# A two-layer encoder with 32 experts per layer: the experts' token lists are loaded three experts ahead, and two small steps beside the experts change place

## The chip, the cores and the metric

The kernel runs on one core of one Trainium2 chip. A core has a matrix engine (TensorE, PE in the profile; its weight loads are PEld), a vector engine (VectorE, DVE), a scalar engine (ScalarE, ACT), a general engine (GpSimd, POOL) that also issues the indirect DMAs, and SyncE (SP), which issues the large loads. Each engine works off its own instructions in order; semaphores tie them together. The metric is the device time of one execution in microseconds: 5532.35 us before the change, the median of three runs (5514.12, 5542.82, 5532.35).

## The reference

The input is x, 4096 tokens of 1024 float32. Two layers follow one another. Each has a mixer over positions (layer 0: retention in two directions and windowed attention; layer 1: a Fourier transform over positions and channels), then a layer norm, then a mixture of experts, then a layer norm:

```
x   = layer_norm(alpha * x + mixer(x))
g   = top-1 of 4 groups (softmax of x @ w_coarse + b_coarse)
e   = top-2 of the 8 experts of group g (x @ w_fine + b_fine)
ffn = sum over the two experts: gate_e * ((silu(x @ w_gate_e) * (x @ w_up_e)) @ w_down_e)
x   = layer_norm(alpha * x + ffn)
```

There are 32 experts per layer, each with a hidden width of 512. Every token goes through two of them, so an expert sees some 128 to 430 tokens.

## The kernel before

The program runs two sweeps for the mixer of layer 0, then the experts of layer 0 (class `Experts`, layer 0), the Fourier mixer, and the experts of layer 1, with the class `Done` beside them. The change touches only `Experts` and `Done`.

**What the lists are.** The router leaves in DRAM, for each expert, a list of (row of the token, gate). `Experts.index` (L1507) loads the list of one expert into a small tile `idx` by a plain DMA issued from GpSimd; there is a ring of three such tiles. `Experts.gather` (L1514) fetches 128 token rows into `xg` by an indirect DMA whose offsets are in `idx`. `Experts.scatter` (L1605) adds a finished tile `yo` to the rows of the accumulator `acc_d` in DRAM, again with offsets of `idx`; two scatters follow each other only when the earlier one has landed.

**One expert.** `Experts.expert(e)` (L1613) writes out the order of work by hand. It begins with what is left of expert e-1: the second half of its output product for tile 1 and that tile's scatter (the function `pending`). Then it issues `index(e+1)` and the gathers of expert e+1 on GpSimd. Then come the 32 steps of `gate_up` (L1540): four blocks j of eight steps k, each step six matmuls of expert e's weights `w` against the transposed tokens `xt`. Block j writes the PSUM tile `pgu[j % 2]`, so block 2 needs block 0 to have been read, and block 3 (its first weights are `w6`) needs block 1 to have been read: by a ScalarE silu (L1556) and a VectorE product (L1557) into `hid`. Then `down` (L1564) multiplies the hidden values by the output weights, and between its products the transposes of expert e+1's gathered tokens (`trans`, L1518) are woven in.

**The weights.** Each expert has 12 chunks of 512 KB. SyncE loads them into a ring of four `raw` tiles; `split` (L1492) turns a chunk into a high part (ScalarE) and a low part (VectorE) at fixed steps: 0, 2, 4, 6 for the current expert's last four chunks, then steps 1 and 3 of blocks 1 to 3 for the next expert's chunks 0 to 5 (`w0` to `w5`), and the rest within `down`. ScalarE and VectorE work in order, so a late chunk holds whatever stands behind its split.

**Finished tokens (layer 1 only).** `Done` normalizes and writes out tokens whose experts are all behind. Its steps are placed by (expert, step) in `Done.plan` (L1244). In experts 0 to 7, `count` (L1279) copies four columns to the bf16 tile `lb` on VectorE; `ranks` (L1283) multiplies them on TensorE and works out places `ddsti` on VectorE; `write` (L1299) issues four indirect DMAs on GpSimd, each of which waits for the one before it to land. From expert 8 on, `Done.gather` fetches a finished tile, `stats` (VectorE, then two small GpSimd instructions, L102 and L1332) finds mean and deviation in `dst`, `scale` (ScalarE, L1335) waits for them, `gain` (GpSimd, L1338), `bias` (VectorE) and `store` (GpSimd) follow.

Of the kernel before, what the change touches and what calls it, by code (L numbers as in the profile page):

```python
# [9 lines left out]
I32 = mybir.dt.int32  # L10
# [4 lines left out]
P = 128  # L15
# [4 lines left out]
E = 32  # L20
# [1192 lines left out]
class Done:  # L1213
# [30 lines left out]
    def plan(s):  # L1244

        put = lambda e, h, f, *a: s.at.setdefault(e, {}).setdefault(h, []).append(lambda: f(*a))
        for e in range(8):
            for h, f in ((9, s.count), (16, s.ranks), (22, s.write)):
                put(e, h, f, 4 * e)
        put(7, 23, s.counts)  # L1250
        put(8, 20, s.load)

        def tile(k, i, b, eg, hg, ec, hc, at=(0, 8, 10, 14, 16)):
            ix = s.ix[:, sum(CAPS[:k]) + i, :]
            put(eg, hg, s.gather, ix, b)
            for d, f in zip(at, (s.stats, s.scale, s.gain, s.bias, s.store)):
                put(ec, hc + d, f, ix, b)
        for k in range(3):
            es = range(8 * k + 8, 8 * k + 16 if k < 2 else 29)
            for i in range(CAPS[k]):  # L1260
                j, e = i // len(es), es[i % len(es)]
                tile(k, i, e % 2 + 2 * j, e, 28 + j, e + 1, 8 + 4 * j)
        for i in range(2):
            tile(3, i, 2 * i, 30, 12 + i, 30, 20 + 3 * i)
        for i, b in enumerate((1, 3, 4)):
            tile(3, 2 + i, b, 30, 28 + i, 31, 1 + 2 * i, (0, 5, 6, 11, 12))
        for i in range(2):
            tile(4, i, 2 * i, 31, 12, 31, 18 + i, (0, 8, 14, 24, 25))
# [168 lines left out]
class Experts:  # L1437
# [8 lines left out]
    def __init__(s, T, layer, sp, pp):  # L1446
        s.T, s.nc, s.tc = T, T.nc, T.tc
        s.layer, s.slots = layer, SLOTS[layer]
        w = max(s.slots)
        s.listed = sum(T.listed[layer][-2:], [])  # L1450
        s.x, s.acc, s.lst, s.cnt = T.x1_d[layer], T.acc_d[layer], T.lst_d[layer], T.cnt[layer]
        s.wgu, s.wd = T.A["wgu"][layer], T.A["expert_w_down"][layer]
        pair = lambda n, sh: (sp.tile(sh, F32R, name=n + "h"), sp.tile(sh, F32R, name=n + "l"))
        s.raw = [sp.tile([P, 1024], F32, name=f"raw{i}") for i in range(s.NRAW)]
        s.w = [pair(f"w{i}", [P, 1024]) for i in range(12)]
        s.nt = -(-w // P)
        s.xg = [sp.tile([P, D], F32, name=f"xg{i}") for i in range(s.nt)]
        s.xt = pair("xt", [P, 8, w])
        s.idx = [sp.tile([P, s.nt, 2], I32, name=f"idx{i}") for i in range(3)]
        s.lidx = sp.tile([P, 2, 2], I32, name="lidx")  # L1460
        s.hid = [sp.tile([P, w], F32, name=f"hid{i}") for i in range(2)]
        s.ht = pair("ht", [P, 4, w])
        s.tail = sp.tile([P, 4, 128], F32R, name="tail")
        s.yo = [sp.tile([P, D], F32, name=f"yo{i}") for i in range(2)]
        s.ylo = sp.tile([64, 512], F32, name="ylo")
        s.over = sp.tile([1, E], F32, name="over")
        s.cap = sp.tile([1, E], F32, name="cap")
        s.more = sp.tile([1, 1], I32, name="more")
        s.pgu = [pp.tile([P, 2, 512], F32, name=f"pgu{i}") for i in range(2)]
        s.pt = [pp.tile([P, 512], F32, name=f"pt{i}") for i in range(2)]  # L1470
        s.py = [pp.tile([P, 512], F32, name=f"py{i}") for i in range(2)]
        s.nload = s.nsplit = 0
        s.c = dict.fromkeys(("pt", "py"), 0)
        s.done = Done(T, sp, s.acc, s.nxt, s.raw) if layer else None
# [26 lines left out]
    def rows(s, e, t):  # L1501
        return max(0, min(P, s.slots[e] - t * P))
# [2 lines left out]
        return range(-(-s.slots[e] // P))  # L1505

    def index(s, e):  # L1507
        ix = s.idx[e % 3]
        n = len(s.tiles(e))
        d = s.nc.gpsimd.dma_start(ix[:, 0:n, :], s.lst[e * LS:e * LS + n * P, :].rearrange("(t p) c -> p t c", p=P))  # L1510
        if e == 0:
            s.T.after(d, s.listed)
# [99 lines left out]

    def expert(s, e):  # L1613

        ix, size = s.idx[e % 3], s.slots[e]
        rows = lambda t: s.rows(e, t)
        late = [f for t in s.tiles(e) if t > 1 for f in s.trans(t, rows(t))] if e else []
        pend, s.pend = s.pend, None
        if pend:
            at = {}  # L1620
            for i, f in enumerate(late):
                at.setdefault(i if len(late) > 2 else 2 * i + 1, []).append(f)
            pend(at)
        more = e + 1 < E
        steps = []
        if more:
            ix2 = s.idx[(e + 1) % 3]
            s.index(e + 1)
            for t in s.tiles(e + 1):
                s.gather(ix2, t, s.rows(e + 1, t))  # L1630
            steps = [f for t in range(2) for f in s.trans(t, s.rows(e + 1, t))]
        at = [{2 * i: [s.split] for i in range(4)}]
        at += [{1: [s.split], 3: [s.split]} for _ in range(3)]
        side = {h: list(f) for h, f in s.done.at.get(e, {}).items()} if s.done else {}
        if e == 2:
            side.setdefault(13, []).append(s.excess)
        if s.last(e):
            for t in s.tiles(e):
                side.setdefault(20, []).append(lambda t=t: s.done.fetch(ix, t, t, rows(t)))
        for h in [h for h in side if h < 32]:  # L1640
            at[h // 8].setdefault(h % 8, []).extend(side.pop(h))
        for j in range(4):
            s.gate_up(j, size, at[j])
        steps = [s.split] + steps[:3] + [s.split] + steps[3:]
        at = {2 * i: [f] for i, f in enumerate(steps[:4])}
        for h in [h for h in side if h < 40]:
            at.setdefault(h - 32, []).extend(side.pop(h))
        yo = s.yo[0]
        if s.last(e):
            m = rows(2)  # L1650
            yo0 = s.done.x[4]
            s.down(yo0, ix, 0, at=at)
            s.done.adds(yo0, 0, P, 0)
            if m:
                s.down(s.yo[1], ix, 2, m)
            side = [f for h in sorted(side) for f in side[h]]
            for f in side:
                f()
            first0, second0 = s.done.final_steps(yo0, 0, P)
            first0()  # L1660
            if m:
                s.done.adds(s.yo[1], 2, m, 2)
                first2, second2 = s.done.final_steps(s.yo[1], 2, m)
                first2()
            s.down(yo, ix, 1, rows(1), last=True)
            second0()
            s.done.final(yo, 1, rows(1))
            if m:
                second2()
            return  # L1670
        order = [0, *(t for t in s.tiles(e) if t > 1)]
        for i, t in enumerate(order):
            y = s.yo[(len(order) - i) % 2]
            s.down(y, ix, t, rows(t), at=at if t == 0 else {})
            s.scatter(y, ix, t, rows(t))
        s.down(yo, ix, 1, rows(1), (0,), at={i: [f] for i, f in enumerate(steps[4:])})
        for h in sorted(side):
            for f in side[h]:
                f()

        def pending(at={}):
            s.down(yo, ix, 1, rows(1), (1,), at)
            s.scatter(yo, ix, 1, rows(1))
        s.pend = pending
# [39 lines left out]
    def run(s):  # L1724
        nc, tc = s.nc, s.tc
        s.pend = None
        with tc.manual_schedule(engines=COMPUTE | {POOL}):
            s.index(0)
            nc.gpsimd.memset(s.ylo, 0.0)
            nc.scalar.copy(s.tail[0:64].rearrange("p k c -> p (k c)"), s.ylo)  # L1730
            nc.scalar.copy(s.tail[64:128].rearrange("p k c -> p (k c)"), s.ylo)
            for t in s.xg:
                nc.gpsimd.memset(t, 0.0)
            for t in s.tiles(0):
                s.gather(s.idx[0], t, s.rows(0, t))
            for _ in range(8):
                s.split()
            for t in s.tiles(0):
                for f in s.trans(t, s.rows(0, t)):
                    f()  # L1740
            nc.sync.dma_start(s.cap, s.T.A["c_slots"][s.layer:s.layer + 1, :])
            if s.done:
                s.done.setup()
            for e in range(E):
                s.expert(e)
            if s.pend:
                s.pend()
            if s.done:
                s.done.finish()
            s.rest()  # L1750
# [146 lines left out]
```

## Time and profile before

| what | value |
|---|---|
| median of three runs | 5532.35 us |
| the profiled execution's own time | 5520.84 us |
| its span (first to last instruction) | 5519.2 us |
| PE busy | 5089.8 us (92%) |
| DVE busy | 3413.6 us (62%) |
| ACT busy | 2382.1 us (43%) |
| POOL busy | 1636.5 us (30%) |
| mean granted TensorE clock | 0.957 |
| bytes moved | 907.96 MB, mean 165 GB/s |

The span is 1.6 us shorter than the execution's own time. Busy times are sums over the whole program; the stages differ, so the rows further down go by stage. The experts of layer 0 run from about 2100 to 3420 us of the span, those of layer 1 from about 4048 to 5476 us.

### The profile page before, as it was taken

Reading aid. Unit: us, or ns where it says so; the run is one execution under the profiler, and the core shown is the slowest. Engines: PE = TensorE matmul, PEld = TensorE weight load, DVE = VectorE, ACT = ScalarE, POOL = GpSimd, SP = SyncE. Lnnn points to the kernel's source line nnn. Section 1 sums busy time; section 2 is a strip of 40 time slices with the busy share of each in tenths; the row PEclk is TensorE's granted clock in tenths of the full one; section 3 lists DMA queues with packets and bytes.
Section 4 is the critical chain, followed back from the end, with each engine's and each line's share of the span. In section 5 each row is a group of like instructions: output and inputs, shape, how many; then the busy total and the mean of one; then the engine's idle time right before and its main releaser. Section 6 shows DMA issues by size and latency. Waiting matters only on the chain. (4 is left out here: it accounts for less than half of the span.)

```text
span 5519.2 us, 85268 instructions
## 1 busy us (share of the span) xinstructions
PE 5089.8 (92%) x32364; PEld 4607.6 (83%) x32364; DVE 3413.6 (62%) x7398; ACT 2382.1 (43%) x4310; POOL 1636.5 (30%) x1556
## 2 busy tenths in 40 slices
PE   9999999799999996999999997889859999999986
PEld 7888888599999986989999896779858888888876
DVE  6777777566666665555544453759855565555555
ACT  4555555322222214555545453643245455555443
POOL 1111111033333332221212121845632333332335
PEclk9999999799999998999999998999869999999998
DMA  4212121433333326777766675866467877777664
GB/s 155 63 59 67 55 67 48 146 103 103 113 100 112 104 89 213 237 218 221 206 183 197 185 238 160 257 206 219 174 195 206 216 226 245 213 212 207 205 212 146
DMA packets 312312, 907.96 MB, mean 165 GB/s; under 512 B 48596, under 2 KB 76420, under 8 KB 311796
## 3 DMA queue, kind: packets, MB, share of 16 engines
q1 hardware_dynamic: 249780, 709.44, 38.4%
q0 software_dynamic: 62096, 192.82, 15.0%
q8 instruction: 259, 4.24, 0.3%
q14 instruction: 177, 1.45, 0.1%
HBM read 678.13 MB, written 226.39 MB: 164 GB/s over the span
## 5 line engine op out<-in xcount | busy, mean ns | idle before, releaser
L1606 POOL DMA_INDIRECT acc_d<-yo,idx x154 | 275.5, 1789 | 1210.8 <-ACT yo L1587 723.4
L83 PE MATMUL pj<-w1h,xh 128*128 128x512 f32 (+1 forms) x1024 | 396.7, 387 | 7.0 <-ACT w1h L78 6.5
L84 PE MATMUL pj<-w1l,xh 128*128 128x512 f32 (+1 forms) x1024 | 378.4, 370 | 2.4 <-DVE w1l L79 2.3
L85 PE MATMUL pj<-w1h,xl 128*128 128x512 f32 (+1 forms) x1024 | 377.0, 368 | 0.0
L1515 POOL DMA_INDIRECT xg<-x_d,idx x157 | 167.7, 1068 | 508.3 <-issue 292.9
L133 PE MATMUL pt<-ident,xg 128*128 128x128 f32 x1256 | 201.5, 286 | 109.7 <-DMA xg<-x_d,idx 61.5
L133 PEld LDWEIGHTS pt<-ident,xg 128*128 128x128 f32 x1256 | 163.4, 148 | 163.7 <-DMA xg<-x_d,idx 64.0
L79 DVE TENSOR_TENSOR xtl<-pt,xth 128x512 fp32r<-128x512 f32 (+12 forms) x314 | 184.9, 598 | 180.8 <-ACT xth L78 179.3
L83 PE MATMUL pj<-w2h,xh 128*128 128x384 f32 (+1 forms) x768 | 265.3, 346 | 9.4 <-DVE rb L212 9.1
L83 PE MATMUL po<-woh,cath 128*128 128x354 f32 (+1 forms) x768 | 262.5, 342 | 2.9 <-ACT cath L78 2.0
L1587 ACT ACTIVATE yo<-py,idx 128x512 f32<-128x512 f32 (+6 forms) x256 | 175.8, 687 | 206.6 <-PE py L85 192.3
L85 PE MATMUL po<-woh,catl 128*128 128x354 f32 (+1 forms) x768 | 254.6, 332 | 5.4 <-DVE catl L79 4.2
L78 ACT ACTIVATE hth<-hid 128x256 fp32r<-128x256 f32 (+11 forms) x256 | 104.6, 408 | 351.8 <-DVE hid L1557 343.5
L84 PE MATMUL pj<-w2l,xh 128*128 128x384 f32 (+1 forms) x768 | 251.8, 328 | 3.4 <-DVE w2l L79 3.3
L84 PE MATMUL po<-wol,cath 128*128 128x354 f32 (+1 forms) x768 | 253.3, 330 | 0.0
L85 PE MATMUL pj<-w2h,xl 128*128 128x384 f32 (+1 forms) x768 | 251.2, 327 | 0.0
L78 ACT ACTIVATE ph<-tr 128x384 fp32r<-128x384 f32 (+1 forms) x256 | 122.6, 479 | 286.4 <-PE tr L133 283.6
L1556 ACT ACTIVATE hid<-pgu 128x272 f32<-128x272 f32 (+22 forms) x256 | 97.5, 381 | 336.2 <-PE pgu L1552 330.7
L79 DVE TENSOR_TENSOR pl<-tr,ph 128x384 fp32r<-128x384 f32 (+1 forms) x256 | 139.0, 543 | 134.3 <-ACT ph L78 130.5
L85 PEld LDWEIGHTS pj<-w1h,xl 128*128 128x128 f32 x1024 | 194.3, 190 | 32.7
L1557 DVE TENSOR_TENSOR hid<-hid,pgu 128x272 f32<-128x272 f32 (+22 forms) x256 | 107.8, 421 | 177.2 <-ACT hid L1556 171.7
L78 ACT ACTIVATE xth<-pt 128x512 fp32r<-128x512 f32 (+12 forms) x314 | 161.1, 522 | 126.9 <-PE pt L133 125.3
(507 smaller groups left out, 18688.3 us busy)
## 6 DMA issues: line engine op xcount, KB each, us to landing
raw<-in_wgu SPq DMA_DIRECT2D x512, 512.0 KB
raw<-in_expert_w_down SPq DMA_DIRECT2D x256, 512.0 KB
xraw<-in_xT SPq DMA_DIRECT2D x64, 512.0 KB
acc_d<-xacc SPq DMA_DIRECT2D x64, 512.0 KB
x<-x_d SPq DMA_DIRECT2D x32, 530.0 KB
xres<-in_x SPq DMA_DIRECT2D x32, 512.0 KB
x_d<-tres SPq DMA_DIRECT2D x32, 512.0 KB
fx<-acc_d SPq DMA_DIRECT2D x32, 512.0 KB
```

Of the source, the lines that this page charges most:

```text
L78: self.nc.scalar.activation(hi, src, AF.Copy)
L79: self.nc.vector.tensor_sub(lo, src, hi)
L83: mm(out, xh, wh, start=start, stop=False)
L84: mm(out, xh, wl, start=False, stop=False)
L85: mm(out, xl, wh, start=False, stop=stop)
L133: self.nc.tensor.transpose(pt[:, k * P:(k + 1) * P], src[:, k * P:(k + 1) * P], self.ident)
L1515: s.nc.gpsimd.indirect_dma_start(out=s.xg[t][0:m, :], out_offset=None, in_=s.x, in_offset=bass.IndirectOffsetOnAxis(ap=ix[0:m, t, 0:1], ax ...
L1556: nc.scalar.activation(hid, ps[:, 0, 0:n], AF.Silu)
L1557: nc.vector.tensor_mul(hid, hid, ps[:, 1, 0:n])
L1587: s.nc.scalar.activation(yo[0:m, w], py[i][0:m, :], AF.Copy, scale=gate)
L1606: s.nc.gpsimd.indirect_dma_start(out=s.acc, out_offset=bass.IndirectOffsetOnAxis(ap=ix[0:m, t, 0:1], axis=0), in_=yo[0:m, :], in_offset=No ...
```

## The change

The list of expert e+3, no longer that of expert e+1, is loaded in `expert(e)`, and it is issued ahead of what is left of expert e-1, no longer behind it. The ring has five tiles. The lists of experts 1 and 2 are loaded before the first expert, behind the gathers of expert 0. In `Done.plan`, `count` moves from step 9 to step 2, `ranks` from 16 to 20, `write` from 22 to 26, and the last `counts` from 23 to 27, so that `lb` is made 18 steps ahead of its use (before: 7).

```diff
-            for h, f in ((9, s.count), (16, s.ranks), (22, s.write)):
+            for h, f in ((2, s.count), (20, s.ranks), (26, s.write)):
                 put(e, h, f, 4 * e)
-        put(7, 23, s.counts)
+        put(7, 27, s.counts)
...
-        s.idx = [sp.tile([P, s.nt, 2], I32, name=f"idx{i}") for i in range(3)]
+        s.idx = [sp.tile([P, s.nt, 2], I32, name=f"idx{i}") for i in range(5)]
...
     def index(s, e):
-        ix = s.idx[e % 3]
+        ix = s.idx[e % 5]
...
     def expert(s, e):
-        ix, size = s.idx[e % 3], s.slots[e]
+        ix, size = s.idx[e % 5], s.slots[e]
         rows = lambda t: s.rows(e, t)
         late = [f for t in s.tiles(e) if t > 1 for f in s.trans(t, rows(t))] if e else []
         pend, s.pend = s.pend, None
+        if e + 3 < E:
+            s.index(e + 3)
         if pend:
...
         if more:
-            ix2 = s.idx[(e + 1) % 3]
-            s.index(e + 1)
+            ix2 = s.idx[(e + 1) % 5]
             for t in s.tiles(e + 1):
                 s.gather(ix2, t, s.rows(e + 1, t))
...
             for t in s.tiles(0):
                 s.gather(s.idx[0], t, s.rows(0, t))
+            s.index(1)
+            s.index(2)
             for _ in range(8):
                 s.split()
```

## Rows read from the trace of the kernel before

**Rows 1.** Busy time by stretch: length, engines' busy us (instructions), granted clock, DMA share, GB/s.
```profile
2120.00:3380.00 1260.00, 1250.90 (x8478) 1140.06 (x8478) 648.11 (x843) 651.96 (x991) 242.04 (x179) 1.00 0.71 208
4060.00:4400.00 340.00, 313.08 (x2234) 288.18 (x2232) 189.85 (x336) 174.17 (x269) 94.71 (x77) 0.93 0.75 209
4400.00:5475.00 1075.00, 990.85 (x6273) 885.28 (x6274) 626.21 (x821) 526.57 (x804) 379.59 (x348) 0.96 0.72 213
```
**Rows 2.** PE's waits, 4060 to 5476 us: releaser, us in total, times, longest.
```profile
PE py L83 <- ACT hth L78: 51.1, 15, 9.8
...
PE pt L133 <- DMA xg<-x_d,idx: 16.0, 4, 8.0
PE pt L1287 <- DVE lb L1281: 11.6, 5, 4.1
```
**Rows 3.** Timeline of ACT, DVE, PE in layer 1, expert 1: start, length, idle before.
```profile
4106.50 1.06 ACT L78 ACTIVATE w0h<-raw 128x1024 fp32r<-128x1024 f32 x1 [2.83 <-DMA raw<-in_wgu]
4108.73 0.17 DVE L1281 CAST lb<-last 128x24 bf16<-128x24 f32 x1
4112.80 0.17 DVE L1297 CAST ddsti<-ddst 128x4 int32<-128x4 f32 x1
4108.95 0.18 PE L1287 MATMUL pt<-lb,trib 128*128 128x24 bf16 x1 [3.92 <-DVE lb L1281]
```
**Rows 4.** Busy time by stretch, just behind that stall.
```profile
4112.00:4128.00 16.00, 16.00 (x77) 16.00 (x77) 6.22 (x13) 3.34 (x6) 4.49 (x4) 0.50 0.67 225
```
**Rows 5.** Timeline of POOL in layer 1, expert 1.
```profile
4106.07 1.47 POOL L1606 DMA_INDIRECT acc_d<-yo,idx  x1 [7.54 <-DMA acc_d<-yo,idx]
4107.03 1.36 POOL L1510 DMA_DIRECT2D idx<-lst_d  x1
4113.47 1.55 POOL L1515 DMA_INDIRECT xg<-x_d,idx  x1 [5.08 <-issue]
...
4116.57 1.02 POOL L1301 DMA_INDIRECT done_d<-rows,ddsti  x1 [0.30 <-issue]
```
**Rows 6.** Timeline of POOL, DVE, ACT in layer 1, a later expert with finished tokens.
```profile
5240.83 1.46 POOL L1510 DMA_DIRECT2D idx<-lst_d  x1
5251.51 1.04 POOL L1515 DMA_INDIRECT xg<-x_d,idx  x1 [9.22 <-DMA idx<-lst_d]
...
5255.00 0.59 POOL L102 TENSOR_TENSOR dst<-dst,mhalf 128x1 f32<-128x1 f32 x1
5247.71 0.15 DVE L101 TENSOR_SCALAR dst<-dst 128x1 f32<-128x1 f32 x1
5255.99 1.24 ACT L1335 ACTIVATE dx<-dx,dst 128x1024 f32<-128x1024 f32 x1 [7.36 <-POOL dst L1332]
```
**Rows 7.** Waits: PE's from 5235 to 5270 us, then ACT's from 4430 to 5480 us.
```profile
PE py L83 <- ACT hth L78: 9.8, 1, 9.8
ACT dx L1335 <- POOL dst L1332: 80.3, 20, 7.4
```
**Rows 8.** Layer 0, experts 0, 9 and 30: block 1 read (DVE), first w6h matmul (PE).
```profile
2127.84 0.35 DVE L1557 TENSOR_TENSOR hid<-hid,pgu 128x192 f32<-128x192 f32 x1 [1.17 <-ACT hid L1556]
L1550 PE MATMUL pgu<-xth,w6h x8: 272/274/278, 2132.6 to 2135.0; 128*128 128x192 f32 x8
2450.32 1.06 ACT L78 ACTIVATE w1h<-raw 128x1024 fp32r<-128x1024 f32 x1 [4.87 <-DMA raw<-in_wgu]
2452.56 0.35 DVE L1557 TENSOR_TENSOR hid<-hid,pgu 128x192 f32<-128x192 f32 x1
L1550 PE MATMUL pgu<-xth,w6h x8: 273/274/277, 2453.3 to 2455.7; 128*128 128x192 f32 x8
3328.50 0.36 DVE L1557 TENSOR_TENSOR hid<-hid,pgu 128x208 f32<-128x208 f32 x1
L1550 PE MATMUL pgu<-xth,w6h x8: 270/274/278, 3330.0 to 3332.4; 128*128 128x208 f32 x8
```
**Rows 9.** Timeline of POOL in layer 0, expert 9.
```profile
2451.54 2.01 POOL L1515 DMA_INDIRECT xg<-x_d,idx  x1 [8.81 <-issue]
```

## The prediction

> **What bounds the kernel now.** I read the busy time by stretch first. In the experts of layer 0 TensorE is busy 1250.9 of 1260 us at a granted clock of 1.00: nothing is to be had there, and anything that holds TensorE up costs in full [rows 1]. In the experts of layer 1 it is busy 313.1 of 340 and 990.9 of 1075 us, 111.1 us idle, at a clock of 0.93 and 0.96 [rows 1]. So the case is decided in layer 1, and layer 0 can only lose. The mixers are not touched.
>
> TensorE's own waits in layer 1 come next: 51.1 us for `hth` (the hidden values), 16.0 for gathered tokens `xg`, 11.6 for `lb` [rows 2]. These three, 78.7 us, are what the change can reach. The timelines of the engines that release them say why they are late.
>
> `lb`: in expert 1 ScalarE idles 2.83 us for a weight chunk before it splits `w0`, the split's low part and, right behind it, the cast to `lb` come late on VectorE (4108.73), and TensorE stands 3.92 us at the product of `ranks` [rows 3]. It then runs a whole 16 us at a clock of 0.50, 1.2 instead of 2.4 GHz [rows 4].
>
> `xg` and `hth`: on GpSimd the scatter of the expert before is issued at 4106.07, the list's load at 4107.03, and the gather that needs the list only at 4113.47 [rows 5]. Later in the layer the gap is longer: list at 5240.83, gather at 5251.51 [rows 6]. Behind the gathers in GpSimd's order stand the two small instructions that finish `dst`. VectorE's share of the second `dst` was ready at 5247.86, GpSimd began the first at 5255.00, and ScalarE stood 7.36 us before the scaling that needs it [rows 6]. ScalarE is in order, so the next splits and the next silu are late too, and TensorE loses 9.8 us at the down product [rows 7]. ScalarE lost 80.3 us in 20 such waits [rows 7].
>
> **The change, part by part.**
>
> *Casting `lb` earlier.* A step has two matmuls of line 1550. The eight with `w6h` start from 2453.3 to 2455.7, seven gaps in 2.4 us, so a step is 0.69 us [rows 8]. Seven steps ahead is 4.8 us, 18 is 12.3; the longest wait was 4.1 [rows 2]. The cast (0.17 us) now stands behind the splits of steps 0 and 2, not behind `w0`. Bounds: 0 to 11.6 us gained; I take 11, because only a chunk later by 8 us more would bring the wait back.
>
> *Ranks and writes four steps later.* That is 2.7 us later by the same step, and the ten small VectorE instructions now stand behind the splits of steps 17 and 19. Who waits for them is GpSimd's first write. In expert 1 `ddsti` was ready at 4112.97 and the write went out at 4116.57, straight behind the gathers: GpSimd was 3.6 us later than its operand [rows 3, 5]. With gathers some 6 us earlier the write waits for `ddsti` instead, at about the old time, and what is queued behind it (three writes, the next scatter) keeps its time. Bounds: 2.7 us lost to 3.6 gained on GpSimd per expert, 0 on TensorE, which has no wait for scatters [rows 2]. I take 0.
>
> *The list's load, moved.* Its issue takes 1.4 us [rows 5, 6]. It now stands ahead of the scatter, which idles 7.54 us for the earlier scatter anyway [rows 5]; it hides there, and without that cover it would cost GpSimd 1.4 us per expert. What it waits for, the ring's tile, was last read two experts before. Before the first expert of a layer three lists go out ahead of the next gather instead of one, at most 3 us more in a queue that is needed 20 us later: 0. Its bytes are the same; they now travel ahead of a scatter and no longer behind it. SyncE issues nothing new and is passed by nothing: its chunks go out in the same order, each when a split has freed its tile.
>
> *The gathers.* They go out 6.4 us earlier in expert 1 and 10.7 us earlier in the later one (difference of the two issue times) [rows 5, 6]. The tokens do not arrive that much earlier: they follow the scatter through the same queue, whose transfer was part of the old wait. The four `xg` stalls are 16.0 us, the longest 8.0, not shown one by one; bounds 0 and 16, and I take 12, since most of the advance beats most of the stalls.
>
> *`dst` and ScalarE.* The two GpSimd instructions follow the gathers, so they are bound by VectorE: ScalarE's 7.36 us go almost wholly, while the stall that they made is 9.8, so 75% of it [rows 6, 7]. Not all 15 stalls are of that kind. Bounds 0 and 51.1; I take 70%, 36 us. What is late next is the chain itself: scaling, splits and the slow products behind them on ScalarE and VectorE, which I count in the remaining 15 us.
>
> *The clock.* At 0.93 and 0.96, 313.1 and 990.9 us of busy time hold 21.9 + 39.6 = 61.5 us of lost pace; layer 0, nearly without stalls, holds none [rows 1]. Per us of idle time that is 61.5 / 111.1 = 0.55. The 59 us of stalls that I take away give back 33 more. Bounds 0 and 61.5.
>
> *What the earlier gathers collide with.* In layer 0 block 3 must find block 1 read. From the end of VectorE's product to the first `w6h` matmul there are 4.4 us in expert 0, 0.4 in expert 9 and 1.1 in expert 30; of the 31 experts 14 have under 2.5 us [rows 8]. What shortens it is the chunk `w1`, which ScalarE waited 4.87 us for and got at 2450.32, while the gather went out at 2451.54 [rows 8, 9]. The new gather travels in the stretch before, where that chunk is still coming. Two gathers are 1.05 MB, 5.0 us at layer 0's 208 GB/s [rows 1]. So `w1` comes 0 to 5.0 us later; half of it, 2.5 us, is my value, the middle of two ends with no row nearer to either. Summed over the 14 experts what is missing then is 17.7 us. Layer 1 moves its bytes at the same pace (209 and 213 GB/s) but ends most blocks with room; I charge a third, 6. Together 24 us, with no clock on top: layer 0's short stalls leave it at 1.00 [rows 1]. Here the Trainium skill ("DMA: Bandwidth & Descriptors", section "Queues, rings and completion order") speaks against the change: each DMA engine takes turns between the queues that have work, packet by packet. No row here separates the queues' packets; by that rule raw chunk and gather share evenly while both are there, and the whole 5.0 us would be lost, which is the second rival below.
>
> *What shows next.* With 59 us less idle time ScalarE meets its chunks sooner; I charge 8 us.
>
> **Sum.** 11 + 12 + 36 + 33 - 24 - 8 = 60 us less than the profiled execution's 5520.8: 5461. The median stands 11.5 us above that execution, so 5472.
>
> **Rivals.** (A) *The wait only changes its place.* The gathers leave early but wait behind the scatter in their queue, the `xg` stalls stay, and ScalarE, no longer held by `dst`, is held by its chunks; or the gather is released by a newer list of the same queue, so that the change doesn't do what it says. For it: the chunk in expert 1 was 2.83 us late before any gather of that expert went out [rows 3, 5]. Against it: `dst` needs no DMA at all. Then only `lb` is won, 11 + 6 of clock, less 10 of collision: 5525.
>
> (B) *Slower: the gathers take the weights' time.* If `w1` comes the full 5.0 us later, what is missing in layer 0 sums to 59 us over 31 experts, in layer 1 to a third, 20; stalls of that length cost clock as layer 1's do, so 79 x 1.55 = 122 us against the 92 won: 5532 + 30, or 5562. For it: the margins of 0.4 and 1.1 us [rows 8]. Against it: eight of the 31 margins are 5 us or more, the lists' own load leaves that stretch, and the scatter ahead of the gathers holds them back. It decides from about 4.3 us of delay, where 45 us in layer 0, a third more and the clock outweigh 92.
>
> (C) *All of it.* 78.7 us of stalls with 43.6 of clock and no collision: 122 us, 5410.
>
> **How the numbers follow.** Forecast 0.58, its own range 5425 to 5505; A 0.20; B 0.12; C 0.10. A measurement of this kernel tells about 0.5% from no change, so faster means under 5505: nearly all of the forecast (0.55), C, and 0.03 of A: 0.68. Same: 0.03 of the forecast, 0.15 of A, 0.01 of B: 0.19. Slower: 0.02 of A and 0.11 of B: 0.13. The range reaches from half of C, 5415, over A, into B, 5545.
>
> **What would show it.** Right: GpSimd's gather straight behind the scatter (idle 0.3 us, not 5 to 9); no wait for `lb`; ScalarE's 80.3 us before L1335 under 20; `hth` waits of TensorE near 15 us; the clock in layer 1 at 0.97 or more. Layer 0's stretch 15 to 25 us longer, with waits of `pgu` on `hid`, would show the collision at my size; none would make 5.0 us, and the range's upper part, wrong. The forecast is wrong if `hth` waits stay above 35 us, or if layer 0 loses more than layer 1 gains.

## The result, and the profile after

The changed kernel takes 5465.84 us, the median of four runs (5445.98 to 5478.56); the kernel before took 5531.82, the median of four as well. The ratio is 0.9885, with an interval of 0.9857 to 0.9912. The forecast was 5472 us.

To see what each part gave, the stretches must begin and end at the same work. The next two views give the busy time by stretch, cut at first matmuls with `w0h` (columns as in [rows 1]): layer 0 from expert 0's to the last expert's; in layer 1 expert 0, experts 1 to 7, and expert 8 to the last expert's. Before:

```profile
2113.30:3348.30 1235.00, 1225.98 (x8274) 1117.83 (x8273) 645.93 (x837) 646.65 (x980) 239.03 (x178) 1.00 0.72 212
4059.70:4093.50 33.80, 33.80 (x252) 31.26 (x251) 20.51 (x41) 19.40 (x33) 4.58 (x4) 0.97 0.73 228
4093.50:4371.80 278.30, 255.85 (x1784) 234.18 (x1783) 153.61 (x277) 140.56 (x218) 78.53 (x63) 0.92 0.75 204
4371.80:5445.90 1074.10, 987.15 (x6280) 881.12 (x6279) 617.01 (x805) 530.62 (x808) 369.44 (x336) 0.96 0.73 216
```

And after:

```profile
2109.00:3359.70 1250.70, 1232.55 (x8275) 1118.70 (x8274) 646.50 (x837) 646.47 (x980) 244.70 (x176) 0.99 0.71 210
4071.10:4124.00 52.90, 52.90 (x253) 50.18 (x252) 20.85 (x41) 19.22 (x33) 7.92 (x7) 0.60 0.49 143
4124.00:4394.10 270.10, 247.90 (x1784) 223.28 (x1783) 153.28 (x277) 138.73 (x218) 75.02 (x63) 0.97 0.81 210
4394.10:5403.40 1009.30, 970.17 (x6280) 870.94 (x6279) 618.47 (x805) 531.45 (x808) 394.45 (x331) 0.98 0.76 230
```

Length less PE's busy time is its idle time. Layer 0: 15.7 us longer, 9.1 of it idle, the rest a slightly lower clock. Experts 1 to 7: 8.2 shorter at equal idle time, so by the clock alone (0.92 to 0.97). Experts from 8 on: 64.8 shorter, 47.8 less idle time and 17.0 less busy time. Expert 0 of layer 1: 19.1 longer with no idle time at all, at a clock of 0.60. What lies ahead of layer 0, which the change doesn't touch, was 4.3 shorter. The sum is -42.5, and the spans differ by 42.3 (5519.2 to 5476.9).

That is less than the 66.0 between the medians. Expert 0 of layer 1 accounts for most of the difference; the experiments say what it is.

PE's waits in layer 1 of the kernel after, from the first `w0h` matmul on (columns as in [rows 2]):

```profile
PE pt L133 <- DVE xtl L79: 34.9, 19, 4.4
PE py L83 <- ACT hth L78: 14.4, 14, 3.4
PE pgu L1550 <- DVE hid L1557: 5.9, 2, 3.2
PE pgu L1550 <- ACT xth L78: 3.0, 2, 2.0
PE pt L133 <- DMA xg<-x_d,idx: 2.5, 1, 2.5
```

Against [rows 2], `hth` went from 51.1 to 14.4, `xg` from 16.0 to 2.5 and `lb` from 11.6 to nothing. Part came back: in the same stretch before, `xtl` had 27.7, `hid` 1.2 and `xth` 1.1.

ScalarE's wait for `dst` (80.3 us, 20 times, in [rows 7]) is down to one:

```profile
ACT dx L1335 <- POOL dst L1332: 2.3, 1, 2.3
```

How that came about is seen in a late expert with finished tokens, on POOL and ACT (columns as in [rows 6]):

```profile
5254.65 2.62 POOL L1606 DMA_INDIRECT acc_d<-yo,idx  x1 [4.54 <-ACT w9h L78]
5257.56 1.28 POOL L1515 DMA_INDIRECT xg<-x_d,idx  x1 [0.30 <-issue]
...
5261.67 1.49 POOL L102 TENSOR_TENSOR dst<-dst,mhalf 128x1 f32<-128x1 f32 x1 [0.31 <-DVE dst L101]
...
5266.23 0.27 POOL L1332 TENSOR_SCALAR dst<-dst 128x1 f32<-128x1 f32 x1
5266.31 1.23 ACT L1335 ACTIVATE dx<-dx,dst 128x1024 f32<-128x1024 f32 x1
```

In [rows 6] the gather stood 9.22 us for its list, and GpSimd's part of `dst` behind it with it. Here the gather leaves 0.30 us behind the scatter, GpSimd waits 0.31 us for VectorE's part of `dst`, which in [rows 6] had lain ready for 7 us, and ScalarE's scaling has no idle time ahead of it. Over all gathers, what GpSimd waited for ahead of line 1515 (us, times; the two largest), before and then after:

```profile
  issue: 292.9, 124
  DMA idx<-lst_d: 125.1, 16
```
```profile
  issue: 43.1, 142
  DMA idx<-lst_d: 13.3, 2
```

### The profile page after: what moved, and what is told of

It is laid out like the page before. It is cut to its first block, busy times and chain, and to the rows that moved or that the text cites. A ratio compares the mean times of both kernels' runs of the same rounds, so it can differ in the third digit from the quotient of the medians.

```text
span 5476.9 us, 85272 instructions
## 1 busy us (share of the span) xinstructions
PE 5087.8 (93%) x32364; PEld 4605.3 (84%) x32364; DVE 3411.8 (62%) x7398; ACT 2380.9 (43%) x4310; POOL 1668.6 (30%) x1556
## 5 line engine op out<-in xcount | busy, mean ns | idle before, releaser
L83 PEld LDWEIGHTS pj<-w1h,xh 128*128 128x128 f32 x1024 | 194.3, 190 | 23.6 <-ACT w1h L78 8.0
L84 PEld LDWEIGHTS pj<-w1l,xh 128*128 128x128 f32 x1024 | 194.3, 190 | 20.5 <-DVE w1l L79 6.3
```

Of the source, the lines that this page charges most:

```text
L83: mm(out, xh, wh, start=start, stop=False)
L84: mm(out, xh, wl, start=False, stop=False)
```

## The experiments

Ratios are to the kernel before on the same chip. "After" as a basis means the changed kernel. To read the times, one table, in us, each row from one trace cut as above (layer 0; in layer 1 experts 0, 1 to 7, and 8 to the last):

| kernel | layer 0 | expert 0 | 1 to 7 | from 8 |
|---|---|---|---|---|
| before | 1235.0 | 33.8 | 278.3 | 1074.1 |
| ranks_only | 1236.7 | 54.2 | 282.8 | 1078.9 |
| dst_first | 1239.3 | 45.7 | 285.1 | 1025.7 |
| lists_layer1 | 1241.5 | 53.8 | 278.4 | 1004.7 |
| lists_only | 1245.5 | 53.9 | 280.0 | 1006.0 |
| place_only | 1251.9 | 53.0 | 275.5 | 1006.5 |
| after | 1250.7 | 52.9 | 270.1 | 1009.3 |
| after_again | 1250.9 | 53.8 | 274.9 | 1001.5 |
| cast_only_early | 1249.2 | 34.1 | 274.5 | 1000.9 |
| hold_layer0 | 1232.5 | 53.9 | 271.4 | 1012.1 |
| hold_cast | 1232.0 | 54.3 | 261.1 | 1004.9 |
| warm_first | 1230.2 | 33.1 | 270.9 | 1005.4 |
| warm_after | 1249.5 | 33.0 | 277.7 | 1011.5 |
| warm_cast | 1234.1 | 33.7 | 276.9 | 1006.5 |

**after_again**: the changed kernel as it is, beside the others.

> The changed kernel once more, for a second trace. Its first trace has three parts against before: layer 0's experts +15.7 us (1235.0 to 1250.7 from the first to the last expert's first matmul), experts 0 to 7 of layer 1 +10.9, experts 8 to 30 of layer 1 -64.8. Theory A (the +10.9 is chance of the clock: expert 0 ran at a granted clock of 0.50 for some 44 us in that trace): expert 0 of layer 1 takes 34 to 37 us here, not 53, while the +15.7 and the -64.8 come again within 5 and 10 us. Theory B (the change itself slows expert 0, by three list loads ahead of the gather): expert 0 takes 50 us or more again. Both: ratio to before 0.985 to 0.992.

Measured: 5472.80 us, 0.9868 (0.9844 to 0.9891). With the first measurement, 0.9885, the gain is 1.1 to 1.3%. The +15.7 and the -64.8 came again, as +15.9 and -72.6. Expert 0 of layer 1 took 53.8 us, which is the sign of theory B and not the 34 to 37 of theory A. The table speaks against B all the same: ranks_only loads its lists as before and has 54.2, cast_only_early loads them early and has 34.1.

**lists_only**: the lists early, the finished tokens' steps (`count`, `ranks`, `write`, `counts`) as before.

```diff
-            for h, f in ((2, s.count), (20, s.ranks), (26, s.write)):
+            for h, f in ((9, s.count), (16, s.ranks), (22, s.write)):
...
-        put(7, 27, s.counts)
+        put(7, 23, s.counts)
```

> Only the lists' part of the change: lists three experts ahead in a ring of five; count, ranks and write stay at steps 9, 16, 22. Theory A (the time is won in experts 8 to 30 of layer 1, because GpSimd reaches the two small dst instructions without the list's wait and ScalarE is not held): waits of ScalarE for dst under 10 us (before: 80.3), of TensorE for hth near 15 (before: 51.1), ratio to before 0.987 to 0.992; waits for lb of some 5 to 12 us stay. Rival (the ranks' move carries a real share, because the lb waits leave TensorE at half clock): ratio 0.994 or more.

Measured: 5476.57 us, 0.9871 (0.9845 to 0.9897). PE still waits for `lb`; that and `hth` in layer 1:

```profile
PE pt L1287 <- DVE lb L1281: 13.9, 6, 4.3
PE py L83 <- ACT hth L78: 10.8, 10, 3.5
```

ScalarE's wait for `dst` is 2.0 us. So the lists carry the gain, as theory A had it, with a little more wait for `lb` than its 5 to 12 us. The 13.9 us of `lb` and the few us by which experts 1 to 7 are longer than after's (280.0 against 270.1 and 274.9) can't be told from no difference in the time.

**ranks_only**: the other half, on the kernel before.

```diff
-            for h, f in ((9, s.count), (16, s.ranks), (22, s.write)):
+            for h, f in ((2, s.count), (20, s.ranks), (26, s.write)):
...
-        put(7, 23, s.counts)
+        put(7, 27, s.counts)
```

> Only the steps' part of the change: count, ranks and write at steps 2, 20, 26; lists as before. Theory A: the 11.6 us of TensorE's waits for lb go, with at most as much again of clock, ScalarE still waits some 80 us for dst and TensorE some 50 for hth: ratio to before 0.996 to 1.000. The writes now start later in a GpSimd queue that still waits for its lists, so waits for gathered tokens may grow from 16.0 us by up to 8 experts x 2.7 us; that would make it 1.000 to 1.004. Rival (the ranks' move carries half of the gain): 0.994 or less.

Measured: 5540.92 us, 0.9989 (0.9973 to 1.0004). PE's waits in layer 1, without the first experts' start, and ACT's:

```profile
PE py L83 <- ACT hth L78: 51.6, 15, 9.6
...
PE pt L133 <- DMA xg<-x_d,idx: 32.9, 8, 11.2
```
```profile
ACT dx L1335 <- POOL dst L1332: 81.9, 21, 6.9
```

No line for `lb` is left, but `xg` has grown from 16.0 to 32.9. The expectation had named a way: writes that start later hold up the next list and gather. Counted from each expert's first matmul, the gathers issued in experts 2 to 8 of layer 1 leave after 22.6 us on average, before after 19.3. How much of the growth that makes, and how much is the time of `lb` met again at the next late thing, isn't separated. By itself this half is worth nothing in the time.

**lists_layer1**: after, but layer 0 loads its lists where the kernel before did.

```diff
-        if e + 3 < E:
+        if s.done and e + 3 < E:
             s.index(e + 3)
...
+            if not s.done:
+                s.index(e + 1)
             for t in s.tiles(e + 1):
...
-            s.index(1)
-            s.index(2)
+            if s.done:
+                s.index(1)
+                s.index(2)
```

> The changed kernel, but layer 0 loads its lists and gathers in the order of before; layer 1 as changed. Theory A (layer 0's +15.7 us come from gathers that travel while the weight chunks w0 to w3 are still coming): layer 0's experts are back at 1235 us within 3, layer 1 as in the changed kernel, so the ratio is 0.003 below that of the changed kernel in the same rounds: 0.983 to 0.988. Rival (the +15.7 is chance, or comes with the program's layout): layer 0 stays at 1245 us or more and the ratio equals the changed kernel's.

Measured: 5464.87 us, 0.9860 (0.9838 to 0.9883). Layer 0 is 9.2 us shorter than after's, and layer 1 from expert 8 on is as in after. Layer 0's 1241.5 us lie between the theory's 1235 within 3 and the rival's 1245, and the ratio is 0.0008 below after_again's, not 0.003. That speaks for a cost in layer 0 and is, in the time, no more than the scatter.

**dst_first**: before, with the late list left as it is; only the gathers of experts 10 to 30 in layer 1 go behind `dst` in GpSimd's order.

```diff
-            for t in s.tiles(e + 1):
-                s.gather(ix2, t, s.rows(e + 1, t))
+            behind = bool(s.done) and 9 <= e <= 29
+            if not behind:
+                for t in s.tiles(e + 1):
+                    s.gather(ix2, t, s.rows(e + 1, t))
...
+        if more and behind:
+            for t in s.tiles(e + 1):
+                side.setdefault(13, []).append(lambda t=t: s.gather(ix2, t, s.rows(e + 1, t)))
```

> The kernel before with one change of order on GpSimd: in experts 9 to 29 of layer 1 the gathers of the next expert are issued behind the two small dst instructions (at step 13), so that these no longer stand behind the list's wait. Lists, ring, count, ranks and write as before. Theory A (the gain is ScalarE freed from its wait for dst; neither an early list nor early tokens are needed): waits of ScalarE for dst fall from 80.3 to under 15 us, of TensorE for hth from 51.1 to under 25, experts 8 to 30 of layer 1 take 1010 to 1030 us (before 1074.1, changed 1009.3 and 1001.5), layer 0 as before, ratio 0.988 to 0.992. Rival (what pays is that the tokens arrive earlier): they arrive no earlier here, so experts 8 to 30 stay above 1060 us and the ratio above 0.997.

Measured: 5475.27 us, 0.9916 (0.9897 to 0.9935). ACT's wait for `dst`, and PE's in layer 1:

```profile
ACT dx L1335 <- POOL dst L1332: 2.3, 1, 2.3
```
```profile
PE py L83 <- ACT hth L78: 22.7, 11, 5.9
PE pt L1287 <- DVE lb L1281: 16.5, 7, 6.2
```

The list's load stands where it stood, and GpSimd still idles 117.8 us ahead of its gathers in layer 1 (before 244.2, after 33.4, summed over all releasers of line 1515). Yet the stretch from expert 8 on is 48.4 us shorter than before, against 64.8 in after: three quarters of the gain there come from `dst` alone, once it isn't queued behind a gather that waits for its list. That the tokens' earlier arrival pays, the rival, asked for over 1060 us there; it is 1025.7.

**place_only**: before with a ring of three and the list of the next expert, not of the third; its load only moves ahead of what is left of the expert before.

```diff
         pend, s.pend = s.pend, None
+        if e + 1 < E:
+            s.index(e + 1)
         if pend:
...
-            s.index(e + 1)
```

> The kernel before, with the list of expert e+1 still loaded in expert e and a ring of three, but issued ahead of what is left of expert e-1 (ahead of its scatter) and no longer behind it. Theory A (the list's wait was long only because the load stood behind a scatter; its place is what matters, not the three experts): idle time of GpSimd before the gathers under 100 us in all (before 508.3), waits for dst under 15 us, ratio 0.985 to 0.991. Rival (a list loaded in the same expert still lands too late, by 2 us or more per expert): waits for dst 30 us or more, ratio 0.992 or more.

Measured: 5467.15 us, 0.9892 (0.9872 to 0.9912). GpSimd's waits ahead of its gathers:

```profile
  issue: 43.6, 141
  DMA idx<-lst_d: 17.3, 4
```

That is after's 43.1 and 13.3 within 5 us, and ScalarE's wait for `dst` is 2.0. The kernel to compare with is lists_only, which has the same steps: 0.9871, the intervals overlap. Ahead of the scatter is what matters; three experts ahead and a ring of five add nothing that can be seen.

**cast_only_early**: after with `ranks`, `write` and `counts` back at 16, 22 and 23; `count` stays at 2.

```diff
-            for h, f in ((2, s.count), (20, s.ranks), (26, s.write)):
+            for h, f in ((2, s.count), (16, s.ranks), (22, s.write)):
```

> The changed kernel with ranks and write back at steps 16 and 22 and counts at 23; only the cast to lb stays early, at step 2. Theory A (the cast's place removes the lb waits; ranks and writes four steps later gain nothing and cost nothing once the lists are early): no waits for lb, waits for gathered tokens in experts 1 to 7 of layer 1 under 8 us, these experts 268 to 280 us (changed 270.1 and 274.9), the same ratio as the changed kernel within 0.002. Rival (TensorE also has to wait for ranks to stand later, because ScalarE and VectorE lag at step 16): waits of TensorE in ranks or for pt come back with 5 us or more.

Measured: 5447.82 us, 0.9867 (0.9845 to 0.9890), as after_again's 0.9868. PE has no wait for `lb`. That `ranks` and `write` stand four steps later neither costs nor brings anything that the time shows.

**hold_layer0**: after, but in layer 0 the gathers wait until `w1` has been split. They are put at step 12 behind a copy of one element of `w1h`, which can't run earlier.

```diff
-            for t in s.tiles(e + 1):
-                s.gather(ix2, t, s.rows(e + 1, t))
+            if s.done:
+                for t in s.tiles(e + 1):
+                    s.gather(ix2, t, s.rows(e + 1, t))
...
+        if more and not s.done:
+            side[12] = [lambda: s.nc.gpsimd.tensor_copy(s.T.spacer, s.w[1][0][0:1, 0:1].bitcast(F32))]
+            side[12] += [lambda t=t: s.gather(ix2, t, s.rows(e + 1, t)) for t in s.tiles(e + 1)]
```

> The changed kernel, but in layer 0 the gathers wait on GpSimd for the split of chunk w1 of the next expert (a copy of one element of w1's high part stands ahead of them), so that they travel about when they did before; the lists stay three experts ahead. In the changed kernel ScalarE waited 40.2 and 41.1 us for chunk w3 in layer 0 (before 3.6), though w1 came no later (64.7 and 68.6, before 68.6). Theory A (early gathers take the time of chunks w2 and w3; ScalarE and VectorE then reach the transposes late): w3's waits are back under 10 us and layer 0 takes 1235 to 1242 us, ratio 0.002 to 0.003 below the changed kernel's. Rival (the list loads, now ahead of the scatters, delay the chunks): w3's waits stay above 30 us and layer 0 at 1245 us or more.

Measured: 5431.51 us, 0.9834 (0.9810 to 0.9857); layer 0 takes 1232.5 us, 18.2 less than in after. ACT's waits for chunks in layer 0, of before, of after and of hold_layer0 in this order:

```profile
ACT w1h L78 <- DMA raw<-in_wgu: 68.6, 25, 5.0
...
ACT w3h L78 <- DMA raw<-in_wgu: 3.6, 3, 1.9
```
```profile
ACT w1h L78 <- DMA raw<-in_wgu: 64.7, 25, 4.8
...
ACT w3h L78 <- DMA raw<-in_wgu: 40.2, 22, 2.8
```
```profile
ACT w1h L78 <- DMA raw<-in_wgu: 68.6, 25, 5.1
...
ACT w3h L78 <- DMA raw<-in_wgu: 5.8, 6, 2.3
```

The early gathers make `w3` late, 22 times, and not `w1`. The rival, that the list loads ahead of the scatters delay the chunks, falls: these loads stand in hold_layer0 as in after. What reaches PE in layer 0, before, after and in hold_layer0:

```profile
PE pt L133 <- DVE xtl L79: 7.6, 5, 2.2
```
```profile
PE pt L133 <- DVE xtl L79: 16.0, 12, 2.2
```
```profile
PE pt L133 <- DVE xtl L79: 6.8, 7, 2.2
```

**hold_cast**: hold_layer0 with the steps of cast_only_early (its diff).

> The kernel hold_layer0 with ranks, scatters' operands and counts back at steps 16, 22 and 23, the cast to lb staying at step 2: what of the second part of the change is worth something once the lists come early. Theory (only the early cast counts, the four later steps cost and bring nothing, because GpSimd's writes then wait either for the gathers or for their operand): ratio within 0.002 of hold_layer0, 0.9834; no lb wait, xg waits of TensorE behind the initial one under 4 us. Rival (the later steps keep VectorE's small instructions from between the splits that hth needs): hth waits of TensorE in layer 1 up from 12 to over 18 us and ratio 0.986 or more.

Measured: 5427.39 us, 0.9839 (0.9823 to 0.9855); no wait for `lb`, and one for `xg`, the layer's first. As expected by the theory: the early cast is all of the second half that is needed to be rid of the waits for `lb`. The time doesn't show what that is worth: lists_only has these waits and 0.9871, cast_only_early, which differs from it by the cast alone, 0.9867.

**warm_first**: hold_layer0 with 32 products, of which nobody reads the result, at the start of layer 1.

```diff
             for t in s.tiles(0):
+                if s.done:
+                    for c in range(4 * t, 4 * t + 4):
+                        for i in range(4):
+                            nc.tensor.matmul(s.py[i % 2], s.w[c][0][:, 0:P], s.w[c][0][:, 0:512], start=True, stop=True)
                 for f in s.trans(t, s.rows(0, t)):
```

> The kernel hold_layer0 with one addition: at the start of layer 1, where TensorE stood about 26 us before the first gathered tokens and 7 us before the second tile, it multiplies each of the first eight weight chunks four times into a result that nobody reads (32 matmuls, about 7 us of work). Theory (expert 0 of layer 1 runs at half clock because TensorE stood still ahead of it): expert 0 takes 34 to 40 us instead of 53 to 54, the whole kernel 12 to 20 us less than hold_layer0: ratio to the kernel before 0.980 (0.978 to 0.983). Rival (the half clock comes and goes for a reason outside the program, as 3 of 10 traces lack it): expert 0 stays at 53 to 54 us or falls as often as in other kernels, ratio 0.983 to 0.985 as hold_layer0. The stretches of the other experts stay within 8 us of hold_layer0 in both.

Measured: 5419.32 us, 0.9842 (0.9821 to 0.9864). The 26 us ahead of expert 0 of layer 1 and the expert itself, in hold_layer0 and then in warm_first (columns as in [rows 1]):

```profile
4005.00:4031.00 26.00, 3.59 (x17) 3.22 (x17) 10.84 (x11) 10.69 (x13) 11.56 (x12) 0.50 0.63 213
4031.00:4084.90 53.90, 53.90 (x252) 50.93 (x251) 20.85 (x41) 19.17 (x33) 7.51 (x7) 0.59 0.50 142
```
```profile
4003.80:4029.80 26.00, 13.43 (x48) 9.48 (x48) 10.73 (x10) 10.69 (x13) 11.67 (x12) 0.71 0.62 210
4029.80:4062.90 33.10, 33.03 (x252) 30.32 (x252) 20.67 (x41) 19.48 (x33) 4.29 (x4) 1.00 0.69 225
```

The expert takes 33.1 us at a clock of 1.00, no longer 53.9 at 0.59. TensorE still stands 19.7 us ahead of the products, for the split of `w0`; what they fill is the time behind it. The time doesn't show the 20.8 us: its ratio is no better than hold_layer0's, and the 0.978 to 0.983 of the theory is missed. So one trace could also be one of the executions in which the clock was up anyway.

**warm_after** and **warm_cast**: the same 32 products in after, and in hold_cast.

> The kernel after with the 32 unused products at the start of layer 1 (layer 0 as after has it). warm_first's trace had expert 0 of layer 1 at 33.1 us, but its times (ratio 0.9842) were not below those of hold_layer0 (0.9834) and hold_cast (0.9839). Theory (TensorE's standing still ahead of expert 0 makes its half clock, in most but not all executions): expert 0 at 33 to 36 us in this trace, the timed runs at a clock of 0.963 or more each; ratio 0.984 to 0.987, against 0.9868 and 0.9885 for after without the products. Rival (warm_first's trace was one of the executions that escape anyway, 3 of 11 without the products): expert 0 at 53 to 54 us, ratio 0.987 to 0.989.

> The kernel warm_first with ranks, scatters' operands and counts back at steps 16, 22 and 23 as in hold_cast: everything that the runs so far point to in one kernel. Theory (the parts add): expert 0 of layer 1 at 33 to 36 us, the other stretches as hold_cast's within 8 us, ratio 0.980 to 0.983. Rival (the clock of expert 0 falls or not by chance, and the products only cost their 7 us): expert 0 at 53 to 54 us, ratio 0.984 to 0.985.

Measured: 5466.93 us, 0.9848 (0.9832 to 0.9864), and 5452.74 us, 0.9835 (0.9814 to 0.9856), with expert 0 at 33.0 and 33.7 us. One of warm_after's five runs had a mean clock of 0.962, under the 0.963 that the theory wanted of each. All three traces with the products have expert 0 under 34 us; of the eleven without, two have (before 33.8, cast_only_early 34.1), dst_first lies between, and eight are at 53 to 54. The count "3 of 10" and "3 of 11" in the expectations takes dst_first in. The mean clocks of all executions agree: with the products 12 of 15 are at 0.964 or more, in hold_layer0, hold_cast, after and after_again, the same kernels without them, 5 of 20. For the expert's clock the theory stands. In the time the ratio is 0.2 and 0.4% lower than after's (0.9848 against 0.9868 and 0.9885, intervals overlapping) and over hold_cast there is nothing (0.9835 against 0.9839). Expected were 0.980 to 0.983 with the products in hold_cast, and the other stretches within 8 us of hold_cast's: both missed (experts 1 to 7 took 276.9 us, in hold_cast 261.1).

The lowest ratios are those of the kernels that hold layer 0's gathers back: 0.9834, 0.9839, 0.9842 and 0.9835. They can't be told apart, nor from warm_after's 0.9848, and their intervals overlap that of after_again (from 0.9844). That holding the gathers back pays is shown by layer 0 itself: 1230.2 to 1234.1 us in these four, 1245.5 to 1251.9 in the six kernels with early gathers there.

## Why the prediction was right

The forecast was 60 us less than the profiled execution; the traces differ by 42.3. Of these, +19.1 (the clock of expert 0) and -4.3 (ahead of layer 0) are no part of the argument. Without them it is -57.1: stalls 61.8 us gone (forecast 59) and 24.9 of clock (33), less 13.8 of new waits in layer 1 (8 and 6) and 15.7 in layer 0 (18). The terms one by one:

**`lb`, 11 us.** 11.6 to nothing: right. That the ranks' later steps cost nothing is shown by cast_only_early; and the first write leaves at about the old time, as the prediction said: in experts 1 to 7 of layer 1 22.7 us after the expert's first matmul on average, before 22.2. What the prediction didn't say is that with late lists this half brings nothing: in ranks_only `xg` grew by more than `lb` had.

**`xg`, 12 us.** 16.0 to 2.5, or 13.5: right in this trace. In after_again `xg` has 7.3, so the term was 8.7 there.

**`dst` and ScalarE, 36 us.** `hth` 51.1 to 14.4, or 36.7 (in after_again it has 16.6): right, and by the mechanism named, since dst_first alone gets the stretch from expert 8 on 48.4 us shorter with late lists.

**What shows next, 8 us.** `xtl`, `hid` and `xth` rose by 13.8 us together. ScalarE does meet its chunks sooner: its waits for `w0`, `w1`, `w3` and `w5` in layer 1, taken together, rose from 53.5 to 79.7 us. That these make TensorE's new waits is argued, not shown. With the 6 us of the collision that were put on layer 1, 14 were charged there; no row separates the two.

**The clock, 33 us.** This term was too large by 8. The busy time of experts 1 to the last fell from 1243.0 to 1218.1, or 24.9, for 48.0 us less idle time. One reason is that it was taken on the 59 us of stalls and not on what is left after new ones. That the sum comes to 0.52 per us, where 0.55 was assumed, is luck: from expert 8 on 17.0 us came back for 47.8 us less idle time, 0.36 per us, and experts 1 to 7 gave 8.0 at equal idle time (22.45 and 22.20). What is gone there is above all one stretch around the first wait for `lb`, of which [rows 4] shows a part. Before, and the same length from the expert's first matmul on after (columns as in [rows 1]):

```profile
4106.50:4130.00 23.50, 21.05 (x96) 20.72 (x96) 10.75 (x26) 8.31 (x16) 6.38 (x6) 0.50 0.68 227
```
```profile
4124.00:4147.50 23.50, 23.08 (x201) 22.47 (x199) 14.49 (x29) 11.95 (x20) 4.32 (x3) 1.00 0.85 253
```

lists_only and place_only, which still wait for `lb`, have such a stretch too, 20.5 us at 0.50; dst_first, the fourth with such waits, has none over 10.5. ranks_only, without them, is at 0.96 in experts 1 to 7 with 36.2 us of idle time. So no one rate per us of idle time fits both parts of the layer. cast_only_early differs from lists_only by the step of the cast alone: it has no wait for `lb`, no such stretch over 7 us, and takes 274.5 us for experts 1 to 7 at 0.96, where lists_only takes 280.0 at 0.91, one trace each. Experts 1 to 7 and from 8 on are at 0.97 and 0.98, as the prediction asked. [rows 1] could not show that expert 0's clock may be down, since in that execution it was up.

**The collision, 24 us (17.7 in layer 0).** Layer 0 lost 15.7 us in the two traces. Over the six traces with early gathers there it takes 1249.6 us on average, over the four with the order of before 1238.1, so 11.5. The size was nearly right, the step that led to it was wrong, so that the size came out is luck. The step said that the gather delays `w1`, and that block 3 then waits for `hid`. In expert 9 the gather indeed left 9.7 us sooner than in [rows 9] (9.4 counted from the expert's first matmul), but `w1` came as it had. POOL and ACT of the kernel after:

```profile
2441.88 1.33 POOL L1515 DMA_INDIRECT xg<-x_d,idx  x1 [0.30 <-issue]
```
```profile
2450.01 1.06 ACT L78 ACTIVATE w1h<-raw 128x1024 fp32r<-128x1024 f32 x1 [4.84 <-DMA raw<-in_wgu]
...
2455.19 1.06 ACT L78 ACTIVATE w3h<-raw 128x1024 fp32r<-128x1024 f32 x1 [1.16 <-DMA raw<-in_wgu]
```

`w1` was waited for 4.84 us, in [rows 8] 4.87. Where the gather's bytes were is seen in the DMA queues: q1 carries SyncE's chunks, q0 GpSimd's transfers. From 2449 to 2453 us, before and then after (packets, MB, share of the 16 DMA engines):

```profile
q1 hardware_dynamic: 366, 1.31, 80.8%
q0 software_dynamic: 27, 0.03, 4.3%
```
```profile
q1 hardware_dynamic: 227, 0.82, 50.6%
q0 software_dynamic: 225, 0.79, 49.4%
```

The split of `w1` began at 2450.01, so most of this stretch belongs to the chunks after it. In the 6 us ahead of the stretch GpSimd's queue moved 0.58 MB, and before, with no gather issued yet, 0.40: so most of what the queue moved there was the scatter's. The prediction says itself that the tokens follow the scatter through the same queue, but doesn't use it for the collision. This is one expert; why `w1` is spared over the whole layer is not shown. The chunk that pays is `w3`, 36.6 us over the layer, and what TensorE waits for is `xtl`, not `hid` (0.4 us). hold_layer0 shows that the early gathers cause both: with the gathers held back `w3` (5.8 us) and `xtl` (6.8 us) are about where they were before. How `w3`'s delay becomes `xtl`'s is only argued: the product that makes `xtl` needs ScalarE's `xth`, which stands behind the splits on an engine that works in order.

**The rivals.** A (the wait changes its place, 5525) falls with `hth` at 14.4 and ScalarE's wait for `dst` at 2.3. B (gathers take the weights' time, 5562) had layer 0 lose 59 us: 11.5 to 15.7 were lost, and `w1`, where it began, lost nothing. B went by the rule that the Trainium skill states ("DMA: Bandwidth & Descriptors", section "Queues, rings and completion order"), that each DMA engine takes turns between the queues with work. The trace agrees where both queues had work: in the 4 us above they moved 0.82 and 0.79 MB. It doesn't agree with what B made of the rule, neither as to the chunk nor as to the 5.0 us: before, the two queues had taken 85% of the engines' time in that stretch, so that part of the gather's bytes went into room that was free. C (all of it, 5410) is refuted by the 13.8 us of new waits and by layer 0. The nearest to it is hold_layer0, which has the gain of layer 1 without layer 0's loss: 0.9834, or 5440 us of the 5531.82.

**Trace and median.** The terms were read from one execution each. That of before had expert 0 of layer 1 at 33.8 us and that of after at 52.9, so the traces understate the gain by some 19 us, and the medians (66.0) show more of it. That the medians of after include both kinds of execution is an inference, from eleven traces and from the mean clocks of after's four executions, 0.961 and 0.960 in the two longer, 0.965 and 0.964 in the two shorter; no run without a trace shows its experts. That the median came within 6 us of the forecast is therefore partly luck: the profiled execution of after took 5478.56 us, where 5461 was forecast, and in the terms the clock, 8 too large, was made up in part by the stalls, 3 too small, and by the charge for layer 0, 2 too large.

## What to carry over

An engine that works in order gives its own queue's wait to whatever stands behind: look not only at what the waiting instruction feeds, but at the small ones behind it, and at who needs them. Load what an indirect DMA reads ahead of the large transfer of the same queue; one place forward was enough here, and further ahead or more buffers brought nothing that the runs show. In layer 0, which had no slack, the same early transfer only took time from the weights, so place it by stage.

## What was not expected of the hardware

In layer 1 TensorE stands 25.9 us for the first tokens and 7.4 us for the second tile's `xtl`, and in eight of the eleven traces without the unused products it then runs most of expert 0 without a gap at half of its clock. In the kernel after, the stretch is this:

```profile
4071.00:4081.00 10.00, 10.00 (x48) 9.90 (x47) 5.67 (x8) 5.42 (x6) 0.95 (x1) 0.50 0.99 330
...
4101.00:4111.00 10.00, 10.00 (x49) 10.00 (x48) 3.13 (x5) 2.67 (x5) 2.07 (x2) 0.50 0.30 105
4111.00:4121.00 10.00, 10.00 (x50) 8.22 (x50) 3.70 (x7) 4.49 (x9) 1.93 (x3) 0.88 0.28 53
```

TensorE was fully busy from 4071 on and had 1.2 GHz for over 40 us before it came back to 2.4. All eleven start expert 0 at 0.50. In before, dst_first and cast_only_early the clock is up within 4 us, in the other eight after 42 to 45; in cast_only_early the same waits (25.8 and 7.9 us) were followed by 34.1 us for the expert. In dst_first it then falls again, around a wait of 2.1 us for `lb`, which is why its expert 0 lies between. What decides between the two kinds is open.
